# A hybrid decoder block on one core: mean squares from the transposed x, two u blocks in turns, first loads over two queues, scan states with tokens innermost

## The chip, the cores and the metric

One core of one Trainium2 chip runs the whole layer in one launch. The metric is the device time of that launch in microseconds (us), taken as the median of several runs.

## What is computed

The input is 256 tokens of 2048 floats. One residual block and one expert block follow:

```
h = rms_norm(x, attn_norm_g)
proj = h @ w_in[l]                      # u_ssm 1024, q, k, v 1024 each, two gates 2048 each
y_ssm = s5_mixer(u_ssm, ...)            # 64 groups of 16 channels, one complex diagonal state of 64 each,
                                        # bu = u @ bbar; x[t] = abar * x[t-1] + bu[t]; y = Re(c x) + d u
y_att = stick_breaking_attention(rms_norm(q), rms_norm(k), v)
merged = sigmoid(gate_ssm) * (y_ssm @ w_branch_ssm) + sigmoid(gate_att) * (y_att @ w_branch_att)
x = x + merged @ w_out
x = x + hierarchical_moe(rms_norm(x), ...)   # best of 4 groups, best 2 of its 8 experts; 32 experts of 2048 x 512
```

All numbers are float32. The norm divides by the root of the mean square of each token, so it can be applied to a product's rows after the matmul.

## The kernel before, in words

`hybrid_block` writes every engine's program in the order in which the engine runs it. The first part is a list of *blocks* (`b_orient`, `a_orient`, lines 209 to 246), one for 512 columns of a weight matrix: two of u, six of q, k, v, four of the attention gate, four of the attention branch, four of the other gate, two of the GLU, four of the ssm branch, four of the output. A block is cut into *chunks* of 256 of its rows (`subs`), 512 KB of weights each. For a chunk, `dma(i)` (line 124) loads it to `raw` by SP's queue, `split(i)` (line 131) makes two rounded parts of it: `wh` on ACT (a cast) and `wl`, the rest, on DVE. TensorE then multiplies three pairs (`wh` with `xh`, `wh` with `xl`, `wl` with `xh`), four matmuls of 512 columns each, so twelve a chunk. `xh` and `xl` are the same two parts of the transposed x times the norm's weight, made by `x_prep` (line 417). `raw`, `wh` and `wl` have three buffers each.

The loop at line 890 goes over the chunks: it splits chunk i+2, loads chunk i+5, issues the matmuls of chunk i and then lets side programs (generators) put their own instructions behind it, as long as a count of each engine's work allows. `later` puts something off by so many chunks. Four accumulators (`pacc`) serve two blocks at a time.

The side programs that the change touches are these.

- `init_stats` (line 458) makes `rstd`, one over the root mean square per token: it loads x a second time with tokens on the partitions (`xtok`, 2 MB by ACT's queue), squares it on ACT with a running sum, takes the root (`rsqrt`, line 192) and permutes the result by four small matmuls with `perm`, for the u blocks have even tokens in one accumulator and odd ones in the other (`rstdp`). The u blocks are evicted with it (`u_out`) and transposed (`u_tr`).
- `ssm` (line 510) computes the state's coefficients on POOL, clears two large tiles (`BBD`, `CBD`, lines 562 and 563), and fills them on DVE and ACT. It then multiplies u (pairs of tokens) into the states' inputs `Vs`, and after the scan it multiplies the states with `CBD` into `y` (lines 687 to 706): sixteen rounds, each four matmuls with `CB` and eight with `Vs` as the moving side, four column groups of 32 side by side.
- `scan` (line 489) runs over 128 token pairs on DVE. A step is one product and two additions for each of two halves, 64 and 32 elements per partition.

The tile of the states, and the moving side that the y matmuls read from it:

```
Vs = [unit(7 + h, [P, P, 2, 16], F32, f"Vs{h}") for h in range(2)]
pe.matmul(ps[js, 0:P], CBD[:, si - 1, 4 * b + j], X[:, :, si - 1, i],
```

The first P is the partition, the second the token pair, then real and imaginary, then 16 groups. In the preamble (lines 425 to 442) SP issues g1, the first parts of x and the first chunks in turns, and TensorE runs 30 transposes (`W0`) to be warm.

After the blocks come the router and the experts: 32 experts of 12 MB each, in pieces of 2 MB, by SP's queue into a ring of tiles that the first part frees (`load_piece`, line 839).

Of the kernel before, what the change touches and what calls it, by code (L numbers as in the profile page):

```python
# [9 lines left out]
F32 = mybir.dt.float32  # L10
# [7 lines left out]
P = 128  # L18
# [5 lines left out]
BIG = 1.0e4  # L24
U_LATE = (4, 2)
SHORT = 0.1
# [56 lines left out]
def hybrid_block(ctx, tc, A, out):  # L83
# [12 lines left out]
    def slot(h, shape, dt, name):  # L96
        return hp.tile(shape, dt, name=name, tag=f"h{h}")
# [33 lines left out]
    def split(i):  # L131
        if i >= len(subs):
# [20 lines left out]
    rbias = cp.tile([P, 36], F32, name="rbias")  # L153

    ident = cp.tile([P, P], F32, name="ident")
    make_identity(nc, ident)
    nc.scalar.dma_start(small, A["lamdt"])
    ones = cp.tile([P, P], F32, name="ones")
    pool.memset(ones, 1.0)
    uge = cq.tile([P, P], F32, name="uge")  # L160
# [209 lines left out]
    ssq = cp.tile([P, 2, 4], F32, name="ssq")  # L370
    tiny = cq.tile([P, 1], F32, name="tiny")

    def out_fin(n):
# [37 lines left out]

    for bi, (src, nk, begin, mm, fin) in enumerate(blocks):
        for s in range(nk // 2):
            subs.append((src, s, nk, begin, mm, fin))


    def x_prep(k0):
        for k in range(k0, k0 + 2):
            act.activation(xh[:, k], xT[:, k], AF.Copy, scale=g1[:, k:k + 1])
            vec.scalar_tensor_tensor(xl[:, k], xT[:, k], g1[:, k:k + 1], xh[:, k], op0=OP.mult, op1=OP.subtract)  # L420
# [8 lines left out]
    dma(1)  # L429
    x_load(4, 8)  # L430
    dma(2)
    x_load(8, 12)
    wps = acc_tile()
    for _ in range(W0):
        pe.transpose(wps[:, 0:P], ident, ident)
    x_prep(0)
    split(0)
    dma(3)
    x_load(12, 16)
    x_prep(2)  # L440
    split(1)
    dma(4)
    BC = unit(8, [P, 8, 32, 16], F32, "BC")
    xtok = unit(3, [P, 2, D], F32, "xtok")

    def side_loads():
        sp.dma_start(BC[:, 0:4], A["bc"])
        sp.dma_start(dsk, A["ssm_d"])
        sp.dma_start(qkg, A["qkg"])
        sp.dma_start(g2, A["g2"])  # L450
        sp.dma_start(wrg, A["wr"])
        sp.dma_start(rbias, A["rb"])
        prog["side"] = True

    rtmp = cq.tile([P, 3, 2], F32, name="rtmp")
    rsq = cq.tile([P, 2, 2], F32, name="rsq")

    def init_stats():
        yield 0
        for j in range(4):  # L460
            nc.scalar.dma_start(xtok[:, j // 2, 1024 * (j % 2):1024 * (j % 2) + 1024],
                                A["x"][j // 2][:, 1024 * (j % 2):1024 * (j % 2) + 1024])
            yield 0
        for j in range(4):
            xs = xtok[:, j // 2, 1024 * (j % 2):1024 * (j % 2) + 1024]
            act.activation(xs, xs, AF.Square, accum_out=rsq[:, j // 2, j % 2:j % 2 + 1])
            if j % 2:
                yield 0
        vec.tensor_reduce(rtmp[:, 0], rsq, axis=AX.X, op=OP.add)
        vec.tensor_scalar(rtmp[:, 1], rtmp[:, 0], 1.0 / D, EPS, op0=OP.mult, op1=OP.add)  # L470
        rsqrt(rstd, rtmp[:, 1], rtmp[:, 2])
        side_loads()
        yield -1
        for t in range(2):
            ps = bg_tile(t)
            for i in range(2):
                pe.matmul(ps[:, 0:1], perm[i][:, t], rstd[:, i:i + 1], start=(i == 0), stop=(i == 1))
            vec.tensor_copy(rstdp[:, t:t + 1], ps[:, 0:1])
        prog["rstd"] = True
        yield 0  # L480
# [780 lines left out]
```

## Time and profile before

| | |
|---|---|
| median of 3 runs | 1581.26 us (1581.25 to 1585.3) |
| the profiled execution: its own time, its span | 1583.46 us, 1581.8 us |
| TensorE busy, DVE busy, ACT busy | 1269.7, 523.5, 450.8 us |
| bytes read from HBM | 515.24 MB, 327 GB/s over the span |

The span is what the profile covers of the execution; the rest lies around it. A busy TensorE is not TensorE at its best: matmuls overlap and their ends are modelled, so here the distance from one start to the next says more than a length. An fp32 matmul shows as two records, one with rounded operands as one. "Line 77" is the helper through which all instructions of DVE, ACT and TensorE go, so rows are told apart by their tiles.

### The profile page before, as it was taken

The page shows a single profiled execution, that of the slowest core. Times are in us where ns is not written, and L with a number is a line of the kernel's source. Part 1 is how long each engine was busy: PE and PEld are TensorE (multiplying, and loading weights), DVE is VectorE, ACT ScalarE, POOL GpSimd, SP SyncE. Part 2 cuts the span into 40 slices and gives each one's busy share as a digit, 9 for nine tenths or more (in the row PEclk, how much of TensorE's full clock was granted, in tenths as well). Part 3 has the DMA queues.
Part 4 walks back from the last instruction along what each step waited for, and adds up shares of the span by engine and source line. Part 5 has one row for each costly group of instructions (what it writes and reads, how often), then busy time and mean ns, then how long its engine had stood idle before and what let it go on. Part 6 is the DMA issues. An engine that isn't in the chain of part 4 may idle for free. (4 is left out here: it accounts for less than half of the span.)

```text
span 1581.8 us, 25130 instructions
## 1 busy us (share of the span) xinstructions
PE 1269.7 (80%) x10654; PEld 859.6 (54%) x10654; DVE 523.5 (33%) x1342; ACT 450.8 (28%) x769; POOL 42.9 (3%) x112
## 2 busy tenths in 40 slices
PE   8899999999999999977657657657757657657697
PEld 6778888888867888844323323323423323323364
DVE  5664877788845754312002002001002002002001
ACT  5455567554435443221110110110110110110101
POOL 8200000000000000000000000000000000000000
PEclk9999999999999999999987979887988988879899
DMA  8454655566654877899999999999999999999996
GB/s 288 160 161 150 196 155 157 163 193 188 200 183 174 278 265 270 320 410 428 428 426 428 426 426 428 426 426 428 428 426 428 426 427 428 427 426 427 427 427 243
DMA packets 64674, 518.99 MB, mean 328 GB/s; under 512 B 7856, under 2 KB 7856, under 8 KB 40880
## 3 DMA queue, kind: packets, MB, share of 16 engines
q1 hardware_dynamic: 63840, 515.22, 82.7%
q10 hardware_dynamic: 720, 2.15, 0.4%
q8 instruction: 85, 1.39, 0.4%
q14 instruction: 29, 0.24, 0.0%
HBM read 515.24 MB, written 2.10 MB: 327 GB/s over the span
## 5 line engine op out<-in xcount | busy, mean ns | idle before, releaser
L77 PE MATMUL acc<-ew,XY 128*32 128x256 f32 x4096 | 310.7, 456 | 171.7 <-DMA ew<-wgu 171.6
L77 PEld LDWEIGHTS acc<-ew,XY 128*32 128x32 f32 x4096 | 142.4, 126 | 323.3 <-DMA ew<-wgu 186.8
L77 DVE TENSOR_TENSOR wl<-raw,wh 128x1024 fp32r<-128x1024 f32 x200 | 244.4, 1225 | 162.6 <-ACT wh L77 159.1
L77 ACT CAST wh<-raw 128x1024 fp32r<-128x1024 f32 x200 | 209.1, 1051 | 188.2 <-PE acc L77 137.1
L77 DVE TENSOR_TENSOR sg<-sg,acc 128x128 f32<-128x128 f32 x32 | 9.2, 288 | 662.8 <-ACT sg L77 662.8
L77 PE MATMUL acc<-ew,hT 128*32 128x256 f32 (+1 forms) x2080 | 146.9, 431 | 70.8 <-DMA ew<-wd 39.3
L77 ACT COPY XY<-acc 32x256 f32<-32x256 f32 (+1 forms) x260 | 93.4, 359 | 207.3 <-PE acc L77 204.8
L77 PE MATMUL acc<-wh,xh 128*128 128x512 f32 x512 | 145.4, 401 | 3.2 <-ACT wh L77 3.2
L77 PEld LDWEIGHTS acc<-ew,hT 128*32 128x32 f32 x2080 | 73.9, 122 | 136.2 <-issue 50.1
L77 PE MATMUL acc<-wl,xh 128*128 128x512 f32 x512 | 140.7, 392 | 1.1 <-DVE wl L77 1.0
L77 PE MATMUL acc<-wh,xl 128*128 128x512 f32 x512 | 141.2, 393 | 0.0
L77 ACT ACTIVATE sg<-acc 128x128 f32<-128x128 f32 x32 | 8.9, 277 | 419.3 <-PE acc L77 419.3
L77 PEld LDWEIGHTS acc<-wl,xh 128*128 128x128 f32 x512 | 96.4, 189 | 23.0 <-DVE wl L77 2.8
L77 PEld LDWEIGHTS acc<-wh,xl 128*128 128x128 f32 x512 | 97.1, 190 | 20.9
L77 PEld LDWEIGHTS acc<-wh,xh 128*128 128x128 f32 x512 | 93.8, 190 | 22.6 <-ACT wh L77 4.6
L77 PE MATMUL acc<-XY,sc 128*128 128x512 f32 x128 | 62.4, 628 | 14.6 <-ACT XY L77 14.5
L77 PE MATMUL bga<-SL,x 128*128 128x128 f32 x512 | 63.5, 280 | 10.3 <-DVE SL L77 10.3
L77 PEld LDWEIGHTS bga<-SL,x 128*128 128x128 f32 x512 | 59.0, 192 | 22.9 <-DVE SL L77 15.9
L77 DVE TENSOR_TENSOR Vs<-Vs,prod 128x32 f32<-128x32 f32 x508 | 68.1, 189 | 0.0
L77 PE MATMUL acc<-wh,m 128*128 128x512 f32 x256 | 64.6, 392 | 0.0
L77 DVE TENSOR_TENSOR accv<-accv,acc 128x512 f32<-128x512 f32 x56 | 38.5, 688 | 78.1 <-PE acc L77 78.1
L77 PEld LDWEIGHTS acc<-wh,m 128*128 128x128 f32 x256 | 47.6, 188 | 9.5
(228 smaller groups left out, 979.8 us busy)
## 6 DMA issues: line engine op xcount, KB each, us to landing
ew<-wgu SPq DMA_DIRECT2D x123, 2048.0 KB, 39.1
ew<-wd SPq DMA_DIRECT2D x61, 2048.0 KB, 39.1
raw<-win SPq DMA_DIRECT2D x128, 512.0 KB, 4.2
raw<-wout SPq DMA_DIRECT2D x32, 512.0 KB, 4.2
ew<-wgu SPq DMA_DIRECT2D x20, 512.0 KB, 5.5
raw<-wba SPq DMA_DIRECT2D x16, 512.0 KB, 4.7
raw<-wbs SPq DMA_DIRECT2D x16, 512.0 KB, 5.1
raw<-wglu SPq DMA_DIRECT2D x8, 512.0 KB, 5.2
```

The costliest lines, as they stand in the source:

```text
L77: return f(out, *args, **kw)
```

## The change

Each part is in the diff below, which is cut to its core.

1. **Mean squares.** x is not loaded a second time. When `xh` and `xl` of four row blocks are made, ACT squares that part of the transposed x in place, and DVE adds up over the row blocks (`xsq`, three instructions over 8, 4 and 4 of the 16). After chunk 15 (step 14), twelve matmuls with `xsq` as the stationary side and a column of ones add up over the partitions, in both orders of tokens at once, so `perm` is gone. `rstd` and `rstdp` come from one chain.
2. **Turns.** The first twelve chunks go to the two u blocks in turns; then come the last two of each. `x_prep` and the loads of x follow every second chunk. `U_LATE` and the side loads change with it: BC comes in four pieces, and the small tensors earlier.
3. **First loads.** `ones` is made first, on DVE, and a first activation on it has ACT's table loaded; then ACT's queue issues g1, the two halves of the first chunk and `lamdt`, while SP's queue starts with x in halves. `wh` of the first chunk is made by DVE, half by half. The warming transposes are 22.
4. **States.** `Vs` becomes `[P, 2, 16, P]`: the token pairs are innermost. The scan, the eviction into `Vs` and the y matmuls index it accordingly.

```diff
-U_LATE = (4, 2)
+U_LATE = (2, 1)
...
-W0 = 30
+W0 = 22
...
+    ones = cp.tile([P, P], F32, name="ones")
+    vec.memset(ones, 1.0)
+    tiny = cq.tile([P, 1], F32, name="tiny")
+    act.activation(tiny, ones[:, 0:1], AF.Copy)
     ident = cp.tile([P, P], F32, name="ident")
     make_identity(nc, ident)
-    nc.scalar.dma_start(small, A["lamdt"])
-    ones = cp.tile([P, P], F32, name="ones")
-    pool.memset(ones, 1.0)
...
-    perm = []
-    for i in range(2):
-        pt_ = slot(2 * i, [P, 2, P], F32, f"perm{i}")
-        pool.memset(pt_, 0.0)
-        for t in range(2):
-            pool.affine_select(out=pt_[:, t], in_=pt_[:, t], pattern=[[-2, P]], compare_op=OP.not_equal, fill=1.0,
-                               base=P * i - t, channel_multiplier=1)
-        perm.append(pt_)
...
+    turns = [(b, s) for s in range(6) for b in range(nu)] + [(b, s) for b in range(nu) for s in (6, 7)]
+    turns += [(b, s) for b in range(nu, len(blocks)) for s in range(blocks[b][1] // 2)]
+    for b, s in turns:
+        src, nk, begin, mm, fin = blocks[b]
+        subs.append((src, s, nk, begin, mm, fin))
...
-    sp.dma_start(g1, A["g1"])
-    x_load(0, 2)
-    dma(0)
+    raw0 = wp.tile([P, 2, 512], F32, name="raw", tag="raw")
+    src0 = subs[0][0]
+    nc.scalar.dma_start(g1, A["g1"])
+    x_load(0, 1)
+    nc.scalar.dma_start(raw0[:, 0], src0[:, 0])
+    x_load(1, 2)
+    nc.scalar.dma_start(raw0[:, 1], src0[:, 1])
+    dma(1)
...
+    hl_t[0] = tuple(wp.tile([P, 2, 512], F32R, name=n, tag=n) for n in ("wh", "wl"))
+    for k in range(2):
+        x_one(k)
+        vec.tensor_copy(hl_t[0][0][:, k], raw0[:, k])
+        vec.tensor_tensor(hl_t[0][1][:, k], raw0[:, k], hl_t[0][0][:, k], op=OP.subtract)
...
-        sp.dma_start(BC[:, 0:4], A["bc"])
...
+        elif k < 5:
+            sp.dma_start(BC[:, k - 1], A["bc"][:, k - 1])
+        else:
+            sp.dma_start(wrg, A["wr"])
...
+    xsq01 = slot(0, [P, 2, T], F32, "xsq01")
+    xsq = [xsq01[:, 0], xsq01[:, 1], slot(1, [P, T], F32, "xsq2")]
...
-        for j in range(4):
-            nc.scalar.dma_start(xtok[:, j // 2, 1024 * (j % 2):1024 * (j % 2) + 1024],
-                                A["x"][j // 2][:, 1024 * (j % 2):1024 * (j % 2) + 1024])
-            yield 0
-        for j in range(4):
-            xs = xtok[:, j // 2, 1024 * (j % 2):1024 * (j % 2) + 1024]
-            act.activation(xs, xs, AF.Square, accum_out=rsq[:, j // 2, j % 2:j % 2 + 1])
...
+        for at, j, red in ((4, 0, None), (6, 1, (0, 0, 8)), (9, 2, (1, 8, 12)), (12, 3, (2, 12, 16))):
...
+            act.activation(xT[:, 4 * j:4 * j + 4], xT[:, 4 * j:4 * j + 4], AF.Square)
+            if red:
+                vec.tensor_reduce(xsq[red[0]], xT[:, red[1]:red[2]].rearrange("p k t -> p t k"), axis=AX.X, op=OP.add)
+            side_load(1 + j)
...
+        ps = bg_tile(0)
+        for o in range(2):
+            for t in range(2):
+                tt = slice(t, T, 2) if o else slice(P * t, P * t + P)
+                for j in range(3):
+                    pe.matmul(ps[:, 2 * o + t:2 * o + t + 1], xsq[j][:, tt], ones[:, 0:1], start=(j == 0), stop=(j == 2))
+        vec.tensor_scalar(rtmp[:, 1], ps[:, 0:4].rearrange("p (o t) -> p o t", o=2), 1.0 / D, EPS, op0=OP.mult, op1=OP.add)
+        rsqrt(rtmp[:, 0], rtmp[:, 1], rtmp[:, 2])
+        vec.tensor_copy(rstd, rtmp[:, 0, 0])
+        vec.tensor_copy(rstdp, rtmp[:, 0, 1])
...
-                pe.matmul(ps[:, 0:1], perm[i][:, t], rstd[:, i:i + 1], start=(i == 0), stop=(i == 1))
...
-                vec.tensor_tensor(prod[h], X[:, c - 1][:, :, None, :].to_broadcast([P, 2, 2, 16]), coef[h], op=OP.mult)
+                vec.tensor_tensor(prod[h], X[:, :, :, c - 1][:, :, None, :].to_broadcast([P, 2, 2, 16]), coef[h], op=OP.mult)
...
-                    vec.tensor_tensor(X[:, c], X[:, c], prod[h][:, k], op=OP.add)
+                    vec.tensor_tensor(X[:, :, :, c], X[:, :, :, c], prod[h][:, k], op=OP.add)
...
-        Vs = [unit(7 + h, [P, P, 2, 16], F32, f"Vs{h}") for h in range(2)]
+        Vs = [unit(7 + h, [P, 2, 16, P], F32, f"Vs{h}") for h in range(2)]
...
-                src = tiles[i].rearrange("p (a r c) -> p c r a", a=2, r=2)
+                src = tiles[i].rearrange("p (a r c) -> p r a c", a=2, r=2)
...
-                act.copy(Vs[b // 4][:, :, :, j:j + 3:2], src)
+                act.copy(Vs[b // 4][:, :, j:j + 3:2], src)
...
-                            pe.matmul(ps[js, 0:P], CBD[:, si - 1, 4 * b + j], X[:, :, si - 1, i],
+                            pe.matmul(ps[js, 0:P], CBD[:, si - 1, 4 * b + j], X[:, si - 1, i],
...
-                            pe.matmul(ps[js, 1:P], CBD[:, 1 + si, 4 * b + j], X[:, 0:P - 1, si - 1, i],
+                            pe.matmul(ps[js, 1:P], CBD[:, 1 + si, 4 * b + j], X[:, si - 1, i, 0:P - 1],
...
-        if i < 6:
-            x_prep(2 * i + 4)
         split(i + 2)
         dma(i + 5)
+        if i < 12 and i % 2:
+            x_prep(i + 3)
+        if i % 2 == 0 and i < 8:
+            x_load(i + 8, i + 10)
```

How the mean squares move on DVE, at the chunks where rstd is made. `wl` is a chunk's second part, `rtmp` and `rstd` the chain of the norm, `xsq` the new sums. Before:

```order
L77 SCALAR_TENSOR_TENSOR xl<-xT,g_108,xh 128x256 x2
L77 TENSOR_TENSOR wl<-raw,wh 128x1024 x3
L77 TENSOR_REDUCE rtmp<-rsq 128x2
L77 TENSOR_SCALAR rtmp<-rtmp 128x2
L77 RECIPROCAL rstd<-rtmp 128x2
L77 TENSOR_TENSOR rtmp<-rstd 128x2
```

and now:

```order
L77 TENSOR_REDUCE xsq_222<-xT 128x256
L77 TENSOR_TENSOR wl<-raw,wh 128x1024
L77 RECIPROCAL sm<-sm 128x32
L77 TENSOR_TENSOR wl<-raw,wh 128x1024
L77 TENSOR_SCALAR rtmp<-bga 128x4
L77 RECIPROCAL rtmp<-rtmp 128x4
```

The chain of the norm has moved behind the coefficients' reciprocal (`sm`), and starts from a PSUM tile, `bga`, which the matmuls fill.

How TensorE's part of it moves. Before, behind chunk 10:

```order
L77 MATMUL acc<-wl,xh 128x512 x4
L77 MATMUL bga<-rstd,perm_133 128x1
L77 MATMUL bga<-rstd,perm_141 128x1
L77 MATMUL bgb<-rstd,perm_133 128x1
L77 MATMUL bgb<-rstd,perm_141 128x1
L77 MATMUL acc<-wh,xh 128x512 x4
```

and now, behind chunk 15:

```order
L77 MATMUL acc<-wl,xh 128x512 x4
L77 MATMUL bga<-ones,xsq_221 128x1 x2
L77 MATMUL bga<-ones,xsq_222 128x1
L77 MATMUL bga<-ones,xsq_221 128x1 x2
L77 MATMUL bga<-ones,xsq_222 128x1
L77 MATMUL bga<-ones,xsq_221 128x1 x2
L77 MATMUL bga<-ones,xsq_222 128x1
L77 MATMUL bga<-ones,xsq_221 128x1 x2
L77 MATMUL bga<-ones,xsq_222 128x1
L77 MATMUL acc<-wh,xh 128x512 x2
```

Four matmuls that wait for rstd are gone, twelve that wait for the sums are there.

What stands on DVE behind the chain of the norm, where `BC` and `BBD` are the state's coefficients and `uy` the transposed u. Before (wrg had come earlier, and two more copies of uy come later):

```order
L77 COPY uy<-bga 128x512
L77 TENSOR_TENSOR wl<-raw,wh 128x1024
L77 COPY uy<-bgb 128x512
L77 TENSOR_TENSOR wl<-raw,wh 128x1024
L77 TENSOR_TENSOR BC<-BC,sm 128x512 x2
L77 TENSOR_TENSOR BC<-BC 128x512
L77 TENSOR_TENSOR BC<-BC,sm 128x512 x2
L77 TENSOR_TENSOR BC<-BC 128x512
L77 TENSOR_TENSOR wl<-raw,wh 128x1024
```

and now:

```order
L77 TENSOR_TENSOR wrg<-wrg,g_113 128x576
L77 TENSOR_SCALAR qkg<-qkg 128x1
L77 TENSOR_TENSOR BC<-BC,sm 128x512 x2
L77 TENSOR_TENSOR BC<-BC 128x512
L77 TENSOR_TENSOR BC<-BC,sm 128x512 x2
L77 TENSOR_TENSOR BC<-BC 128x512
L77 TENSOR_TENSOR wl<-raw,wh 128x1024
L77 TENSOR_TENSOR BC<-BC,sm 128x512 x2
L77 TENSOR_TENSOR BBD<-BC 64x32x16 x2
L77 TENSOR_TENSOR wl<-raw,wh 128x1024
L77 COPY uy<-bga 128x512
```

wrg has come down to the coefficients, and all four copies of uy stand behind the first of them.

## Rows read from the trace of the kernel before

**Rows 1.** The page: head, and costliest groups (busy us, mean ns, idle before).

```profile
span 1581.8 us, 25130 instructions
...
L77 DVE TENSOR_TENSOR wl<-raw,wh 128x1024 fp32r<-128x1024 f32 x200 | 244.4, 1225 | 162.6 <-ACT wh L77 159.1
```

**Rows 2.** Stretches: us, PE, PEld, DVE, ACT, POOL busy, PEclk, DMA share, GB/s.

```profile
456.00:485.30 29.30, 29.30 (x386) 10.56 (x385) 7.00 (x11) 9.63 (x24) 0.00 (x0) 1.00 0.14 48
485.30:650.00 164.70, 164.47 (x867) 141.08 (x864) 92.87 (x101) 74.87 (x99) 0.00 (x0) 1.00 0.76 263
...
700.00:1500.00 800.00, 524.13 (x5917) 267.76 (x5909) 73.72 (x139) 97.22 (x282) 0.00 (x0) 0.86 1.01 427
```

**Rows 3.** The same table for the stretch of the scan.

```profile
147.00:447.40 300.40, 300.40 (x1375) 250.44 (x1374) 242.82 (x915) 166.09 (x193) 0.00 (x0) 1.00 0.59 183
```

**Rows 4.** Timeline, 35 to 50 us: start, us, engine, line, operation, count [idle before].

```profile
35.87 1.09 PE L77 MATMUL acc<-wh,xl 128*128 128x512 f32 x4
35.94 0.15 DVE L77 TENSOR_REDUCE rtmp<-rsq 128x2 f32<-128x4 f32 x1
36.12 5.63 DVE L77 TENSOR_SCALAR rtmp<-rtmp 128x2 f32<-128x2 f32 x1
...
36.80 1.10 PE L77 MATMUL acc<-wl,xh 128*128 128x512 f32 x4
...
38.22 3.51 POOL L563 MEMSET CBD<- 128x4096 f32 x1
...
43.13 0.98 PE L77 MATMUL bga<-rstd,perm 128*128 128x1 f32 x4 [5.23 <-DVE rstd L77]
...
44.83 2.05 PE L77 MATMUL acc<-wh,xh 128*128 128x512 f32 x4
...
49.43 1.09 PE L77 MATMUL acc<-wh,xh 128*128 128x512 f32 x4
```

**Rows 5.** Timeline, all engines, the first 9 us (same columns).

```profile
4.74 1.28 ACT L77 ACT_TABLE_LOAD   x1 [4.74 <-DMA xT<-xT]
...
7.93 1.20 PE L77 MATMUL acc<-wh,xh 128*128 128x512 f32 x4 [1.67 <-ACT wh L77]
```

**Rows 6.** Timeline of PE, the y stage.

```profile
456.03 0.42 PE L77 MATMUL bga<-uy,CB 32*32 32x128 f32 x8
456.38 1.55 PE L77 MATMUL bga<-Vs,CBD 128*32 128x128 f32 x16
457.87 0.42 PE L77 MATMUL bga<-uy,CB 32*32 32x128 f32 x8
...
485.30 2.18 PE L77 MATMUL acc<-zz,wh 128*128 128x256 f32 x16
```

**Rows 7.** Groups by shape: busy us, mean ns of one, idle before.

```profile
L77 PE MATMUL bga<-Vs,CBD 128*32 128x128 f32 x128 | 12.4, 531 | 0.0
...
L77 PE MATMUL bga<-SL,x 128*128 128x128 f32 x512 | 63.5, 280 | 10.3 <-DVE SL L77 10.3
...
L77 DVE TENSOR_TENSOR Vs<-Vs,prod 128x32 f32<-128x32 f32 x508 | 68.1, 189 | 0.0
...
L77 DVE TENSOR_TENSOR prod<-Vs,coef 128x64 f32<-128x64 f32 x254 | 45.0, 219 | 0.0
...
L77 ACT COPY Vs<-bga 128x512 f32<-128x512 f32 x8 | 4.8, 597 | 18.2 <-PE bga L77 18.2
...
L77 ACT COPY BT<-bga 128x512 f32<-128x512 f32 x4 | 2.4, 588 | 1.6 <-PE bga L77 1.6
```

**Rows 8.** Waits of PE from 50 to 640 us: us in total, times, longest.

```profile
PE acc L77 <- DVE wl L77: 1.0, 3, 0.4
PE acc L77 <- ACT wh L77: 0.6, 1, 0.6
```

**Rows 9.** Timeline of PE, the first expert.

```profile
663.53 1.93 PE L77 MATMUL acc<-ew,XY 128*32 128x256 f32 x32
665.39 3.84 PE L77 MATMUL bga<-SL,x 128*128 128x128 f32 x32
```

More of the change, by code (lines that the diff above doesn't have):

```diff
@@ L273, in hybrid_block @@
         b_orient(A["win"][n], 16, lambda k: xh[:, k], lambda k: xl[:, k], u_fin(n), par=True)
+    nu = len(blocks)
     S = {}
@@ L370, in hybrid_block @@
     ssq = cp.tile([P, 2, 4], F32, name="ssq")
-    tiny = cq.tile([P, 1], F32, name="tiny")
     def out_fin(n):
@@ L410, in hybrid_block, with x_one @@
         b_orient(A["wout"][n], 16, lambda k: S["m"][k // 8][:, 0, k % 8], lambda k: S["m"][k // 8][:, 1, k % 8], out_fin(n))
-    for bi, (src, nk, begin, mm, fin) in enumerate(blocks):
-        for s in range(nk // 2):
-            subs.append((src, s, nk, begin, mm, fin))
+    turns = [(b, s) for s in range(6) for b in range(nu)] + [(b, s) for b in range(nu) for s in (6, 7)]
[3 more added lines that the diff above has]
+        subs.append((src, s, nk, begin, mm, fin))
+    def x_one(k):
+        act.activation(xh[:, k], xT[:, k], AF.Copy, scale=g1[:, k:k + 1])
+        vec.scalar_tensor_tensor(xl[:, k], xT[:, k], g1[:, k:k + 1], xh[:, k], op0=OP.mult, op1=OP.subtract)
     def x_prep(k0):
         for k in range(k0, k0 + 2):
-            act.activation(xh[:, k], xT[:, k], AF.Copy, scale=g1[:, k:k + 1])
-            vec.scalar_tensor_tensor(xl[:, k], xT[:, k], g1[:, k:k + 1], xh[:, k], op0=OP.mult, op1=OP.subtract)
+            x_one(k)
     def x_load(k0, k1):
         sp.dma_start(xT[:, k0:k1], A["xT"][:, k0:k1])
-    sp.dma_start(g1, A["g1"])
-    x_load(0, 2)
-    dma(0)
+    raw0 = wp.tile([P, 2, 512], F32, name="raw", tag="raw")
[6 more added lines that the diff above has]
+    dma(1)
     x_load(2, 4)
-    dma(1)
-    x_load(4, 8)
     dma(2)
-    x_load(8, 12)
+    dma(3)
+    x_load(4, 6)
     wps = acc_tile()
@@ L435, in hybrid_block @@
         pe.transpose(wps[:, 0:P], ident, ident)
[L436 to L440, printed above, removed]
+    nc.scalar.dma_start(small, A["lamdt"])
+    hl_t[0] = tuple(wp.tile([P, 2, 512], F32R, name=n, tag=n) for n in ("wh", "wl"))
+    for k in range(2):
+        x_one(k)
+        vec.tensor_copy(hl_t[0][0][:, k], raw0[:, k])
+        vec.tensor_tensor(hl_t[0][1][:, k], raw0[:, k], hl_t[0][0][:, k], op=OP.subtract)
     split(1)
     dma(4)
+    x_load(6, 8)
+    x_prep(2)
@@ L443, in hybrid_block, with side_load @@
     BC = unit(8, [P, 8, 32, 16], F32, "BC")
-    xtok = unit(3, [P, 2, D], F32, "xtok")
-    def side_loads():
-        sp.dma_start(BC[:, 0:4], A["bc"])
[L448 to L456, printed above, removed]
+    def side_load(k):
+        if k == 0:
+            sp.dma_start(dsk, A["ssm_d"])
+            sp.dma_start(qkg, A["qkg"])
+            sp.dma_start(g2, A["g2"])
+            sp.dma_start(rbias, A["rb"])
+        elif k < 5:
+            sp.dma_start(BC[:, k - 1], A["bc"][:, k - 1])
+        else:
+            sp.dma_start(wrg, A["wr"])
+            prog["side"] = True
@@ L458, in init_stats @@
+    rtmp = cq.tile([P, 3, 2, 2], F32, name="rtmp")
+    xsq01 = slot(0, [P, 2, T], F32, "xsq01")
+    xsq = [xsq01[:, 0], xsq01[:, 1], slot(1, [P, T], F32, "xsq2")]
     def init_stats():
         yield 0
-        for j in range(4):
-            nc.scalar.dma_start(xtok[:, j // 2, 1024 * (j % 2):1024 * (j % 2) + 1024],
-                                A["x"][j // 2][:, 1024 * (j % 2):1024 * (j % 2) + 1024])
-            yield 0
-        for j in range(4):
-            xs = xtok[:, j // 2, 1024 * (j % 2):1024 * (j % 2) + 1024]
-            act.activation(xs, xs, AF.Square, accum_out=rsq[:, j // 2, j % 2:j % 2 + 1])
-            if j % 2:
-                yield 0
@@ L469, in init_stats @@
[L469 to L472, printed above, removed]
-        yield -1
-        for t in range(2):
-            ps = bg_tile(t)
-            for i in range(2):
-                pe.matmul(ps[:, 0:1], perm[i][:, t], rstd[:, i:i + 1], start=(i == 0), stop=(i == 1))
-            vec.tensor_copy(rstdp[:, t:t + 1], ps[:, 0:1])
-        prog["rstd"] = True
@@ L480, in init_stats @@
-        yield 0
+        for at, j, red in ((4, 0, None), (6, 1, (0, 0, 8)), (9, 2, (1, 8, 12)), (12, 3, (2, 12, 16))):
+            while prog["step"] < at:
+                if prog["step"] == 2 and "sl" not in prog:
+                    prog["sl"] = True
+                    side_load(0)
+                yield 0
+            act.activation(xT[:, 4 * j:4 * j + 4], xT[:, 4 * j:4 * j + 4], AF.Square)
+            if red:
+                vec.tensor_reduce(xsq[red[0]], xT[:, red[1]:red[2]].rearrange("p k t -> p t k"), axis=AX.X, op=OP.add)
+            side_load(1 + j)
+            yield 0
@@ new lines, in init_stats @@
+        while prog["step"] < 14:
+            yield 0
+        side_load(5)
+        ps = bg_tile(0)
[5 more added lines that the diff above has]
+        vec.tensor_scalar(rtmp[:, 1], ps[:, 0:4].rearrange("p (o t) -> p o t", o=2), 1.0 / D, EPS, op0=OP.mult, op1=OP.add)
@@ L481, in init_stats @@
+        rsqrt(rtmp[:, 0], rtmp[:, 1], rtmp[:, 2])
+        vec.tensor_copy(rstd, rtmp[:, 0, 0])
+        vec.tensor_copy(rstdp, rtmp[:, 0, 1])
+        prog["rstd"] = True
+        yield -1
         vec.tensor_tensor(wrg, wrg, g2[:, :, None].to_broadcast([P, 16, 36]), op=OP.mult)
```

## The prediction

> **What bounds the kernel now.** Read the page's head first: 1581.8 us of span [rows 1]. The table of stretches then splits it in two. From 700 to 1500 us the DMA engines are busy all the time at 427 GB/s [rows 2]: the expert weights stream, and TensorE waits for them. Before that TensorE is the bound: from 147 to 447 it is busy 300.4 of 300.4 us [rows 3], and from 485.3 to 650 it is busy 164.47 of 164.70 with DMA at a share of 0.76 [rows 2]. The expert stream is issued at fixed places of TensorE's program and into buffers that its program frees, so a microsecond taken from TensorE before 650 should start the stream, and so end the kernel, a microsecond earlier. The question is what the change takes from TensorE. Two places matter.
>
> The first is the start. A chunk of a weight block is twelve matmuls; three groups of four at 0.93 us (35.87 to 36.80 [rows 4]) make 2.80 us. The first chunk begins at 7.93, after ACT had sat until 4.74 for the first x and then loaded a table for 1.28 us [rows 5]. Ten chunks should end 28.0 us later, at 35.9; the tenth ends at 37.73 (36.80 + 0.93), 1.8 us late. Then TensorE does nothing for the blocks until 44.83. The chain is in [rows 4]: a TENSOR_SCALAR of two elements on DVE takes 5.63 us and ends at 41.75, just when the second of POOL's large memsets ends (41.73); rstd hangs on it, TensorE waits 5.23 us for rstd, and eight records of the permutation fill 43.13 to 44.83. The next chunk runs from 44.83 to 49.43, 4.60 us, at half the clock (the four matmuls take 2.05 instead of 1.1). The loss from 7.93 to 49.43 is 41.5 - 11 x 2.80 = 10.7 us.
>
> The second is the y stage, 456 to 485.3, with nothing but y's matmuls [rows 2, 6]. A round is eight CB records (456.03 to 456.38, 0.35 us) and sixteen Vs records (456.38 to 457.87, 1.49 us); an fp32 matmul leaves two records, so that is four matmuls in 0.35 but eight in 1.49, 0.74 per four. One Vs record takes 531 ns, while a matmul of 128 columns by 128 rows with an unbroken moving side (SL,x) takes 280 [rows 7]. The Vs moving side is read with 32 floats between tokens; everything else about it has quick neighbours in the trace.
>
> **The change part by part.**
>
> Start. The first x and the first weights come in halves over two queues, the table is loaded early, and DVE makes the first wh. g1 now stands behind the table load (1.28 [rows 5]) on ACT's queue, so it cannot be much earlier than before, and DVE must do six operations for two halves before the second half is split: two xl, two casts, two wl of half the size of a 1.23 us wl [rows 1]. I put the first matmul at 6.3, with a wait for the second half, and the end of chunk one at 10.0 against 10.73 (7.93 + 2.80): **-0.7** (from -1.8, if nothing waits, to +0.5, if the halves share bandwidth with the second weights). Eight fewer warming transposes cost nothing while they end less than the present 1.67 us ahead of the first matmul [rows 5].
>
> The 2 MB of token-major x are no longer loaded, and the turns between the two u blocks ask for x half as fast. The 1.8 us late by chunk ten go: **-1.8**. What is added in their place is BC in four pieces and small loads, earlier than before; a late one would be seen as TensorE waiting for wh.
>
> The mean squares now end in matmuls behind chunk 15, and the 5.63 us instruction has no successor in the memsets: a TENSOR_REDUCE ran beside that memset in 0.15 us [rows 4], and the first TENSOR_SCALAR of rstd comes near 52 us (10.0, fourteen chunks of 2.80, 2.6 of matmuls), when POOL's memsets (end 41.73, 1.7 us less of perm work ahead of them, lamdt asked for later) are done. The gap goes, 37.73 to 44.83: **-7.1**. The clock stays up, since nothing idles: 4.60 - 2.80, **-1.8**. The added matmuls are 12, so 24 records; eight (bga's four and bgb's) took 1.70 us at half clock [rows 4], 0.107 each at full: **+2.6**. Four squares on ACT replace four of the same size; four elements-by-token sums on DVE (2048, 1024 and 1024 elements, three instructions) are new, at a wl's rate 4.9 us, spread over ten chunks in which DVE has about 2.3 us free per pair of chunks: no cost, and at the worst rate of the rival below (8 us more) some 2 us.
>
> Behind chunk 15 comes a chain: matmuls, TENSOR_SCALAR, square root, seven small DVE operations of about 0.19 [rows 7], then the two evictions that free the accumulators for chunk 17, 0.6 each by ACT's copies of that size [rows 7]. With a hand-over of 0.1 at each change of engine I make it 3.4 us after the matmuls; chunk 16 covers 2.8: **+0.6**. From there to chunk 24 DVE was short already: TensorE waited 1.6 us in four waits [rows 8]. The order puts wrg (576 elements, 0.7) and two more copies of uy (512 elements, 0.6 each, by wl's rate) into that stretch, all ahead of wl chunks, and BBD's copies hold ACT's next cast until DVE is through: **+2.5** (0 to 4). Start in all: -5.7, between -9.5 and -2.
>
> The scan. 254 products and 508 additions [rows 7] now touch elements 512 bytes apart instead of neighbours. No row shows DVE doing this. The nearest is ACT, which writes Vs scattered: 597 ns for 512 elements, and 588 for BT, unbroken [rows 7]. I take it as free; any cost goes first into DVE's 57.6 idle us of this stretch [rows 3].
>
> y. With tokens innermost the moving side is unbroken. Per four Vs matmuls I take CB's 0.35, the nearest in columns and in the four column groups; 32 such groups give 32 x (0.74 - 0.35) = **-12.5**. The lower end is the experts' rate: 32 records of 256 columns in 1.86 us [rows 9], 0.47 per four matmuls, 0.24 for 128 columns: -16. If ACT's sixteen copies and the gelu between them come to decide a round of 1.05 us, some of it is given back; ACT is busy only 9.63 of the 29.3 us now [rows 2], so I expect little; -11.
>
> Sum: -5.7 - 12.5 = -18.2 from 1583.46, which is 1565.3; that execution stands 2.2 above the median of the runs, so **1563**. Its own range goes from 1555 (-9.5 - 16) to 1570 (-2 - 11, and a little DVE).
>
> Against this change speaks a rule on strides. The Trainium skill, Advanced Engine Details and Errata, section SBUF Cachelines, says that accesses which hit a new 16-byte line each time pay. By that rule, the trace agrees for TensorE's Vs reads (531 against 280 ns); for DVE no run here shows it, and there it would work against the new layout.
>
> **The rivals.**
>
> *DVE pays for the stride.* TensorE's excess is (531 - 280)/128 = 1.96 ns for each element out of line. On DVE that is 64 reads in a product, 125 ns x 254 = 32 us, and 32 reads and 32 writes in an addition, 125 ns x 508 = 64 us: 96 us into 57.6 idle ones. TensorE would then wait some 38 us for wl: 1563 + 38 = **1601**, slower. It decides once a scan step (127 of them) costs 0.6 us more ((57.6 + 18.2)/127); with reads alone (64 us) the end is near 1570 still. For it: TensorE's rows. Against: ACT's scattered writes, and that DVE takes 189 ns for 32 elements, mostly fixed.
>
> *The stride is not what slows y*: 128 rows, 32-wide column groups, or accumulation in one bank do. Then only the start remains, 1581.3 - 5.7 = **1576**. Against: the experts do 128 rows in 32-wide groups at 0.24 [rows 9].
>
> *The start gives nothing*: the halves land late, the clock drops in the wait between them (a chunk at half clock cost 1.8), and the DVE backlog behind chunk 15 takes the rest: only y's 12.5, **1569**.
>
> **How the numbers follow.** Forecast 0.75, DVE's stride 0.07, y unchanged 0.08, start lost 0.10. The range 1555 to 1574 holds the forecast and the lost start. No difference means within 0.3%, 4.7 us, about what a measurement can tell: faster lies below 1576.5. The third case sits on that border and is halved: faster 0.75 + 0.10 + 0.04 = 0.89, same 0.04, slower 0.07.
>
> **What would show it.** In the changed profile: the first chunk ending near 10, no gap of TensorE between 10 and 50 beyond the xsq matmuls, granted clock 1.00 throughout the first 50 us; no DVE instruction of 5 us; waits for wh and wl of 3 to 5 us between 55 and 90; Vs,CBD records near 280 ns and the y stage 17 us long; scan additions still near 190 ns; the expert stream at 427 GB/s, beginning 18 us earlier. I am wrong if Vs additions exceed 300 ns, if the y stage stays above 25 us, or if the stream does not move with TensorE.

## The result, and the profile after

The changed kernel takes 1567.36 us in the median (four runs, 1567.0 to 1567.59), the kernel before 1583.17 on the same chip (1581.25 to 1585.3): a ratio of 0.9900, 95% interval 0.9882 to 0.9917. That is 15.8 us less, where 18.2 were forecast; the range held the time. The profiled execution of the changed kernel has an own time of 1567.53 us. From its page, the head and the two groups of the scan on DVE (busy us, mean ns of one, idle before):

```profile
span 1565.8 us, 25150 instructions
...
L77 DVE TENSOR_TENSOR Vs<-Vs,prod 128x32 f32<-128x32 f32 x508 | 76.9, 222 | 0.0
...
L77 DVE TENSOR_TENSOR prod<-Vs,coef 128x64 f32<-128x64 f32 x254 | 56.0, 262 | 0.0
```

The difference of the two spans, 16.0 us, splits without a rest if both timelines of TensorE are cut at the same work. Chunks 2, 11, 12, 17 and 25 start at 10.83, 44.83, 49.43, 64.25 and 89.89 before, and at 13.52, 38.96, 41.76, 58.50 and 88.11 now:

| piece | before | after | moved by | forecast |
|---|---|---|---|---|
| to chunk 2's start | 10.83 | 13.52 | +2.7 | -0.7 |
| chunks 2 to 10, and the gap behind them | 34.00 | 25.44 | -8.6 | -1.8 - 7.1 |
| chunk 11 | 4.60 | 2.80 | -1.8 | -1.8 |
| chunks 12 to 16, with the sums over xsq | 14.82 | 16.74 | +1.9 | +2.6 |
| chunks 17 to 24 | 25.64 | 29.61 | +4.0 | +0.6 + 2.5 |
| chunk 25 to y | 366.14 | 367.04 | +0.9 | 0 |
| the y stage | 29.27 | 14.88 | -14.4 | -12.5 |
| from y's end to the end of the span | 1096.5 | 1095.8 | -0.7 | 0 |

Two groups of u's transposes, 0.36 each, have moved from the fourth piece to the fifth, so these two are better read as +2.6 and +3.3. Nearly all of the net gain is in y. What the start won by the gap that is gone (10.4), it lost again, all but 0.9, in its first chunk, in the matmuls over xsq and behind chunk 16: y starts at 455.15 instead of 456.03, 0.9 us earlier, where 5.7 were forecast.

**The y stage.** The timeline of TensorE in the changed kernel (start, us, engine, line, operation, count), against [rows 6]:

```profile
455.15 0.42 PE L77 MATMUL bga<-uy,CB 32*32 32x128 f32 x8
455.50 0.64 PE L77 MATMUL bga<-Vs,CBD 128*32 128x128 f32 x16
456.07 0.42 PE L77 MATMUL bga<-uy,CB 32*32 32x128 f32 x8
...
470.03 2.18 PE L77 MATMUL acc<-zz,wh 128*128 128x256 f32 x16
```

The sixteen Vs records now fill 0.57 us (455.50 to 456.07), not 1.49; a round takes 0.92. The groups by shape give the record, against 531 ns in [rows 7]:

```profile
L77 PE MATMUL bga<-Vs,CBD 128*32 128x128 f32 x128 | 5.2, 279 | 0.0
...
L77 ACT COPY Vs<-bga 128x512 f32<-128x512 f32 x8 | 4.7, 587 | 18.2 <-PE bga L77 18.2
```

**The first chunk.** TensorE again, from the start:

```profile
1.41 4.95 PE L77 MATMUL acc<-ident 128*128 128x128 f32 x22 [1.41 <-POOL ident masks.py:199]
7.56 1.19 PE L77 MATMUL acc<-wh,xh 128*128 128x512 f32 x2 [1.20 <-DVE wh L77]
9.12 1.19 PE L77 MATMUL acc<-wh,xh 128*128 128x512 f32 x2 [0.37 <-DVE wh L77]
10.11 1.91 PE L77 MATMUL acc<-wh,xl 128*128 128x512 f32 x4
11.81 1.91 PE L77 MATMUL acc<-wl,xh 128*128 128x512 f32 x4
13.52 1.33 PE L77 MATMUL acc<-wh,xh 128*128 128x512 f32 x4
```

The first matmul starts at 7.56, not 6.3, and the chunk runs at about half pace: a group of four takes 1.70 us (10.11 to 11.81), where [rows 4] have 0.93. DVE's first cast, the `wh` of the first half, waits for the weights until 6.98:

```profile
6.98 0.43 DVE L77 CAST wh<-raw 128x512 fp32r<-128x512 f32 x1 [2.61 <-DMA raw<-win]
```

**Chunks 17 to 24.** TensorE's waits from 0 to 460 us, then its timeline and DVE's at the longest of them:

```profile
PE acc L77 <- DVE wl L77: 2.7, 2, 2.4
PE acc L77 <- DVE wh L77: 1.6, 2, 1.2
PE acc L77 <- POOL ident masks.py:199: 1.4, 1, 1.4
PE acc L77 <- ACT wh L77: 1.1, 1, 1.1
```

```profile
82.07 0.61 PE L77 MATMUL acc<-wh,xl 128*128 128x512 f32 x2
85.05 0.73 PE L77 MATMUL acc<-wl,xh 128*128 128x512 f32 x2 [2.37 <-DVE wl L77]
85.63 0.97 PE L77 MATMUL acc<-wh,xh 128*128 128x512 f32 x2
```

```profile
75.36 0.69 DVE L77 COPY uy<-bgb 128x512 f32<-128x512 f32 x1
75.96 0.68 DVE L77 COPY uy<-bga 128x512 f32<-128x512 f32 x1
76.56 1.29 DVE L77 TENSOR_TENSOR BC<-BC,sm 128x512 f32<-128x512 f32 x2
...
80.44 0.68 DVE L77 COPY uy<-bgb 128x512 f32<-128x512 f32 x1
81.04 1.28 DVE L77 TENSOR_TENSOR BC<-BC,sm 128x512 f32<-128x512 f32 x2
82.36 1.39 DVE L77 TENSOR_TENSOR CBD<-BC 64x512 f32<-64x512 f32 x2
83.77 2.36 DVE L77 TENSOR_TENSOR wl<-raw,wh 128x1024 fp32r<-128x1024 f32 x2
```

DVE has no pause here, and the late `wl` stands behind copies of `uy` and the coefficients. The stretches (us, PE, PEld, DVE, ACT, POOL busy, PEclk, DMA share, GB/s) show the backlog, its half clock, the scan and the expert stream:

```profile
85.00:90.00 5.00, 4.95 (x15) 3.91 (x16) 4.92 (x6) 3.26 (x4) 0.00 (x0) 0.66 0.64 206
148.80:451.00 302.20, 302.05 (x1381) 251.39 (x1381) 260.04 (x916) 165.42 (x192) 0.00 (x0) 1.00 0.59 183
...
700.00:1500.00 800.00, 528.19 (x5845) 268.88 (x5837) 73.75 (x139) 97.27 (x281) 0.00 (x0) 0.84 1.01 427
```

After the wait of 2.37 us the granted clock is 0.66 of full between 85 and 90, so part of that stretch runs at 1.2 instead of 2.4 GHz. In the scan DVE has 42.2 idle us left (302.20 - 260.04), where it had 57.6 [rows 3], and TensorE still hardly waits (302.05 of 302.20 us busy). The stream keeps its 427 GB/s, as in [rows 2].

### The profile page after: what moved, and what is told of

The parts are those of the page before. It is cut to its first block, busy times and chain, and to the rows that moved or that the text cites. A ratio compares the mean times of both kernels' runs of the same rounds, so it can differ in the third digit from the quotient of the medians.

```text
span 1565.8 us, 25150 instructions
## 1 busy us (share of the span) xinstructions
PE 1264.8 (81%) x10662; PEld 861.8 (55%) x10662; DVE 543.2 (35%) x1348; ACT 448.7 (29%) x764; POOL 43.1 (3%) x105
## 5 line engine op out<-in xcount | busy, mean ns | idle before, releaser
L77 PE MATMUL acc<-ew,XY 128*32 128x256 f32 x4096 | 304.2, 449 | 166.7 <-DMA ew<-wgu 166.7
L77 DVE TENSOR_TENSOR wl<-raw,wh 128x1024 fp32r<-128x1024 f32 (+1 forms) x201 | 243.9, 1217 | 143.8 <-ACT wh L77 142.8
L77 PE MATMUL acc<-ew,hT 128*32 128x256 f32 (+1 forms) x2080 | 157.0, 454 | 70.0 <-DMA ew<-wd 40.9
L77 DVE TENSOR_TENSOR Vs<-Vs,prod 128x32 f32<-128x32 f32 x508 | 76.9, 222 | 0.0
L77 PE MATMUL acc<-XY,sc 128*128 128x512 f32 x128 | 64.8, 649 | 14.7 <-ACT XY L77 14.6
L77 DVE TENSOR_TENSOR prod<-Vs,coef 128x64 f32<-128x64 f32 x254 | 56.0, 262 | 0.0
```

The source lines that it names most:

```text
L77: return f(out, *args, **kw)
```

## The experiments

The theories: **A**, all of y's gain is the states' layout, and it adds to the rest. On the first chunk: 22 warming transposes are too few. **C**, the 5.63 us of one small DVE instruction in [rows 4] are the two large memsets on POOL, not anything in the norm. **D**, the backlog of chunks 17 to 24 is the four copies of `uy`, which the turns let pile up behind the coefficients on DVE. **E**, what a strided operand costs is decided by whether neighbours share a line of 16 bytes; its rival is that it grows with the distance. Ratios stand against the kernel before, on the same chip.

### The layout alone, and all but the layout

The first kernel is the one before with the new states, the second the changed one with the old states (the lines with `X` and `src` go the same way):

```diff
-        Vs = [unit(7 + h, [P, P, 2, 16], F32, f"Vs{h}") for h in range(2)]
+        Vs = [unit(7 + h, [P, 2, 16, P], F32, f"Vs{h}") for h in range(2)]
```

> The kernel before with the states laid out with tokens innermost, and nothing else of the change. Theory A (the y matmuls' strided moving side cost the time, and it is worth its full price alone): the y stage falls from 29.3 to about 14.9 us, Vs,CBD records to about 272 ns, and the time is 14 to 15 us under the kernel before; the start stays as it was (TensorE idle 5.2 us for rstd). Rival (part of the y gain needs the rest of the change, or the slower scan, 222 instead of 189 ns an addition, costs TensorE waits here): under 10 us of gain, and waits for wl between 147 and 450.

> The changed kernel with the old state layout: mean squares, turns and first loads alone. Theory A (the start gains 10 us at the old gap and gives 9 back at its first chunk and at DVE's backlog): the y stage is 29.3 us again and begins near 455, and the time is within 2 us of the kernel before. Rival (the start is worth its forecast of 5 to 6 us, and the layout less than 12): 5 us or more under the kernel before.

The layout alone: 1570.19 us, 0.9911 (0.9894 to 0.9927), 13.5 less. y takes 14.77 us (457.93 to 472.70), additions 221 and products 262 ns, as in the changed kernel. All but the layout: 1580.95 us, 0.9985 (0.9975 to 0.9995), 2.8 less, with y at 29.27 and records of 531 ns. The two add up to 16.3, against 15.8 together. Theory A holds in the main: the y stage gains its 14.5 us by the layout alone. Both times lie just outside what it asked for (14 to 15 us, and within 2): in the first profile a half-clock chunk behind the gap took 5.26 us instead of 4.60 and y began 1.9 us later, and the rest of the change is worth 2.8 us, with an interval from 0.8 to 4.0.

### Thirty warming transposes

```diff
-W0 = 22
+W0 = 30
```

> The changed kernel with 30 warming transposes again instead of 22. Theory B (the first chunk runs at half clock because the transposes end before the clock has risen): the last transposes run at about 0.11 us each, chunk one takes under 3.5 us from its first matmul instead of 6, ends before 12 instead of 13.5, and the time falls by 1 to 2.5 us. Rival (the first chunk is slow because its halves arrive late, the number of transposes does not matter): chunk one ends at 13.5 or later, and the time is the changed kernel's or up to 2 us more.

1564.89 us, 0.9883 (0.9866 to 0.9899). TensorE's start there:

```profile
1.41 6.23 PE L77 MATMUL acc<-ident 128*128 128x128 f32 x30 [1.41 <-POOL ident masks.py:199]
7.88 0.71 PE L77 MATMUL acc<-wh,xh 128*128 128x512 f32 x2 [0.24 <-DVE wh L77]
9.49 0.71 PE L77 MATMUL acc<-wh,xh 128*128 128x512 f32 x2 [0.90 <-DVE wh L77]
10.04 1.08 PE L77 MATMUL acc<-wh,xl 128*128 128x512 f32 x4
10.96 1.09 PE L77 MATMUL acc<-wl,xh 128*128 128x512 f32 x4
11.90 1.09 PE L77 MATMUL acc<-wh,xh 128*128 128x512 f32 x4
```

The matmuls run at the full pace from the first (0.92 from 10.04 to 10.96), and chunk 2 starts at 11.90 instead of 13.52. From the first matmul the chunk takes 4.0 us, not under 3.5, for 0.90 us of waiting are in it. Over all profiles shown or told of here: with 30 transposes the first four matmuls ran at the full pace in each of seven, with 22 in one of five (the pair layout below). So the pace of the first chunk hangs on the transposes, but not alone: with 22 it differs from execution to execution, and the gain of 2.5 us in the median, whose interval overlaps that of the changed kernel, may be partly chance.

### The first chunk's order on DVE

With 30 transposes, both casts of the first chunk ahead of both `wl`:

```diff
+    x_prep(0)
     for k in range(2):
-        x_one(k)
         vec.tensor_copy(hl_t[0][0][:, k], raw0[:, k])
+    for k in range(2):
         vec.tensor_tensor(hl_t[0][1][:, k], raw0[:, k], hl_t[0][0][:, k], op=OP.subtract)
```

> The changed kernel with 30 warming transposes, and on DVE the two casts of the first chunk's halves ahead of its two wl (after both xl). Theory F (the second half waits in DVE's order, not for its data): the wait between the two halves of chunk one (0.4 to 1.4 us) falls under 0.3, chunk one ends 0.5 to 1 us earlier than with 30 transposes alone (11.9), and the time is 0 to 1 us under that kernel's 1564.9. Rival (the second half's data land late): the second cast waits for DMA, and chunk one ends as with 30 transposes alone.

Chunk 2 starts at 11.15 instead of 11.90, and the wait between the halves is 0.49 instead of 0.90; the second cast then waits 0.83 us for its half of the weights. So the late half has a share. That the order has one is not shown: one of the kernels below, with 30 transposes and the old order, has the same 0.49, and chunk 2 at 11.23. The time shows no gain either: 1565.77 us, 0.9887 (0.9871 to 0.9904), and y starts at 452.53, as with the other order (452.41).

### The memsets of the kernel before, moved

In the kernel before, the clearing of `BBD` and `CBD` goes ahead of the coefficients' chain on POOL; nothing of the norm is touched.

```diff
+        pool.memset(BBD.rearrange("p a b t c -> p (a b t c)"), 0.0)
+        pool.memset(CBD.rearrange("p a b c -> p (a b c)"), 0.0)
         lr, li, ldt = small[:, 0], small[:, 1], small[:, 2]
...
-        pool.memset(BBD.rearrange("p a b t c -> p (a b t c)"), 0.0)
-        pool.memset(CBD.rearrange("p a b c -> p (a b c)"), 0.0)
```

> The kernel before with POOL's two large memsets (BBD, CBD) put ahead of the chain of coefficients instead of behind it, nothing else. Theory C (the memsets alone held the two-element TENSOR_SCALAR for 5.6 us): that instruction takes about 0.2 us, TensorE's 5.2 us wait for rstd and the half clock behind it go, the y stage begins 6 to 9 us earlier and the time falls by 6 to 9 us. Rival (DVE was held by something else, such as ACT's table load or the late x): the instruction still takes over 3 us and the time stays within 2 us.

1579.4 us, 0.9975 (0.9965 to 0.9984), 4.3 less. DVE's timeline, POOL's and TensorE's:

```profile
5.70 6.99 DVE L77 TENSOR_SCALAR iotan<-iota 128x32 f32<-128x32 f32 x1 [5.59 <-POOL iota L184]
...
35.46 0.15 DVE L77 TENSOR_REDUCE rtmp<-rsq 128x2 f32<-128x4 f32 x1
35.65 0.17 DVE L77 TENSOR_SCALAR rtmp<-rtmp 128x2 f32<-128x2 f32 x1
```

```profile
5.68 3.52 POOL L551 MEMSET BBD<- 128x4096 f32 x1
9.14 3.52 POOL L552 MEMSET CBD<- 128x4096 f32 x1
```

```profile
12.78 1.91 PE L77 MATMUL acc<-wh,xl 128*128 128x512 f32 x4 [3.31 <-DVE wl L77]
```

The instruction of the norm is down to 0.17 us and its gap is gone. But another TENSOR_SCALAR, that of `iotan`, starts 0.02 us behind the first memset and ends at 12.69 with the second (9.14 + 3.52 = 12.66): 6.99 us for 32 elements. The hold has only moved, and TensorE waits 3.31 us for it in place of 5.23; the eight matmuls behind that wait run at half pace, and chunk 2 starts at 16.20 instead of 10.83. Theory C holds. From chunk 2 to chunk 12 the kernel wins 9.6 us (29.02 instead of 38.60), and 5.4 of them are lost again in the first chunk: so the gain came out below 6 to 9 us. It also says that the new mean squares were not needed to lose the gap: what they do is to come after the memsets. In the changed kernel the two memsets run from 41.65 to 48.64 beside `wl`, `xl` and `xsq` of the usual lengths (1.23, 0.88, 2.05 us), and no TENSOR_SCALAR or copy of DVE stands there.

The Trainium skill, SBUF — State Buffer, section Who interferes with whom, says that copies, casts and tensor_scalar can run in a mode in which DVE and GpSimd exclude each other at a pair of ports, the later one waiting until the other's instruction ends, and that a tensor_reduce never does. The traces agree, with 5.63 and 6.99 us against 0.15 for the reduce in [rows 4], which ran beside the first memset of the kernel before:

```profile
34.77 3.52 POOL L562 MEMSET BBD<- 128x4096 f32 x1
```

Both held instructions, begun beside the first memset, ended with the second: two memsets in a row let nothing of the kind in between them.

### The copies of uy on ACT

The changed kernel, with one engine exchanged:

```diff
-vec.tensor_copy(uS[:, 4 * c:4 * c + 4], ps
+act.copy(uS[:, 4 * c:4 * c + 4], ps
```

> The changed kernel with the four copies of the transposed u (uy from bga and bgb, 0.68 us each) on ACT instead of DVE. Theory D (DVE's backlog behind the coefficients makes the 2.4 us wait for wl near 85 us and the half clock behind it): DVE is 2.7 us lighter between 65 and 90, the wait falls under 0.5 us, the half clock there goes, the y stage begins 2 to 4 us earlier and the time falls as much. Rival (the late casts of wh on ACT, which wait for data and for BBD's copies, set it): the copies delay ACT's casts by as much as they free DVE, waits for wh take the place of waits for wl, and the time stays within 1 us.

1562.82 us, 0.9866 (0.9849 to 0.9882). From chunk 17's start to chunk 25's it takes 25.37 us (61.33 to 86.70), not 29.61; the longest wait for `wl` is 0.54, and the granted clock is 1.00 from 70 to 90. Theory D holds, but not for the whole 4.2 us. In this profile the matmuls of chunk 16 ran at a granted clock of 0.50 from 56.06 to 61.33, 2.4 us longer; so TensorE came late to the stretch, its wait for ACT's `wh` was 0.21 instead of 1.12, and y starts only 1.7 us earlier (453.48). Where chunk 16 ran at the full pace, the stretch takes 28.60 to 30.05 us with the copies on DVE (four profiles) and 26.14 and 26.21 with them on ACT (the two kernels with both mends below); where it was slowed, 27.74 and 27.76 against 25.37. Like against like, the copies are worth 2.4 to 3.9 us.

The half clock behind the long wait does not always come. Six profiles have the wait of 2.37 or 2.38 us; behind it three run at a granted clock of about 0.50 (the changed kernel, the pairs below, the first chunk's other order), and three, such as that with 30 transposes, have 1.00 and lose nothing more than the wait.

### Two and four groups innermost

The changed kernel, with the states as `[P, 2, 8, P, 2]` and as `[P, 2, 4, P, 4]`: from token to token TensorE goes 8 or 16 bytes, and DVE has two or four neighbours. The scan, the eviction and the order of the four coefficients go with it.

```diff
-        Vs = [unit(7 + h, [P, 2, 16, P], F32, f"Vs{h}") for h in range(2)]
+        Vs = [unit(7 + h, [P, 2, 8, P, 2], F32, f"Vs{h}") for h in range(2)]
```

> The changed kernel with the states as pairs of groups: two groups innermost, then tokens, so TensorE's moving side steps by 8 bytes and DVE touches pairs of neighbours 1024 bytes apart (order of the four coefficients exchanged to fit). Theory E (what counts is whether two accesses in a row fall into one line of 16 bytes): Vs,CBD records stay near 272 ns, the y stage at 15 us, and the scan goes back to about 189 and 219 ns; the time is the changed kernel's within 1 us, for DVE had room. Rival (any step but one float costs TensorE): records of 350 ns or more, y stage over 20 us, time 5 us or more above the changed kernel.

> The same with four groups innermost, so that the moving side steps by 16 bytes and DVE touches runs of four. Theory E: every read of the moving side falls into a new line, the records go back to about 530 ns, the y stage to 29 us, the time to 14 us above the changed kernel; the scan runs at about 189 and 219 ns. Rival (the cost grows with the distance): records between 272 and 530 ns, a y stage between 15 and 29 us.

The pairs: 1566.66 us, 0.9897 (0.9881 to 0.9914), y 15.15 us. The fours: 1573.1 us, 0.9935 (0.9919 to 0.9952), 5.7 above the changed kernel where theory E asked for 14, y 22.03 us. The groups by shape of the pairs, then of the fours:

```profile
L77 DVE TENSOR_TENSOR Vs<-Vs,prod 128x32 f32<-128x32 f32 x508 | 68.9, 191 | 0.0
...
L77 PE MATMUL bga<-Vs,CBD 128*32 128x128 f32 x128 | 5.3, 282 | 0.0
...
L77 ACT COPY Vs<-bga 128x512 f32<-128x512 f32 x8 | 4.9, 610 | 18.0 <-PE bga L77 18.0
```

```profile
L77 DVE TENSOR_TENSOR Vs<-Vs,prod 128x32 f32<-128x32 f32 x508 | 68.0, 188 | 0.0
...
L77 PE MATMUL bga<-Vs,CBD 128*32 128x128 f32 x128 | 8.8, 404 | 0.0
...
L77 ACT COPY Vs<-bga 128x512 f32<-128x512 f32 x8 | 8.6, 1072 | 13.0 <-PE bga L77 12.9
```

One record costs TensorE 279 ns at 4 bytes from token to token, 282 at 8, 404 at 16 and 531 at 128 [rows 7]. Nothing is lost at 4 and 8 bytes, where two reads or more fall into one span of 16; at 16 it costs, and at 128 more. So theory E fits the place where the cost begins, and its rival is right that it then grows. ACT, which writes the same tile, goes with E: 587 and 610 ns at 4 and 8 bytes, 1072 at 16. DVE too: 188 and 191 with four or two neighbours, 222 with none. By the rule on lines that the prediction cited (the Trainium skill, Advanced Engine Details and Errata, section SBUF Cachelines) two hits on a line are enough to hide its latency; the three engines agree on that point, and how much one hit a line costs, by engine, is in these rows.

### Both mends together

The changed kernel with the copies on ACT and 30 transposes, and the same with the pairs:

```diff
-W0 = 22
+W0 = 30
...
-vec.tensor_copy(uS[:, 4 * c:4 * c + 4], ps
+act.copy(uS[:, 4 * c:4 * c + 4], ps
```

> The changed kernel with both mends of the runs so far: the four copies of uy on ACT, and 30 warming transposes. The additive theory: chunks 17 to 24 take 25.4 us from chunk 17's start to chunk 25's, as with the copies alone (29.6 in the changed kernel), and the first chunk ends by 12 at a full clock, as with 30 transposes alone; y begins at 456.0 - 0.9 - 4.2 - 2.7 = 448.2 to 450, and the time is 1567.4 - 4.2 - 2.5 = 1560.7, against 1562.8 with the copies alone and 1564.9 with 30 transposes alone. The rival: an earlier u block only makes the wait for the coefficients or for x longer, so y begins at 452 as in both kernels alone and the time stays at 1562.8 or above.

> The kernel with both mends, and two of the sixteen groups innermost in the states (8 bytes from token to token), which alone brought the scan's additions back to 192 ns at the same TensorE time per record (275). The theory that the scan's extra 19.8 us of DVE are hidden: no difference from the kernel with both mends within 1 us, additions at 192 and products at 218 ns, the y stage 15 us. The rival: with TensorE further ahead of DVE the scan has begun to cost, and the time falls by 1 to 3 us below the kernel with both mends.

Both mends: 1561.6 us (1560.49 to 1561.97), 0.9856 (0.984 to 0.9873), the best version here and 5.8 below the changed kernel. The first chunk ends at 11.76, chunks 17 to 24 take 26.14 us, and y starts in the range that the sum of the two gave:

```profile
449.38 0.42 PE L77 MATMUL bga<-uy,CB 32*32 32x128 f32 x8
```

The transposes add 1.2 us to what the copies give, not 2.5; the intervals of the two kernels overlap, so that they add anything to the time is not shown. With the pairs it is 1561.98 us, 0.9862 (0.9845 to 0.9878), the same within the runs, though additions take 191 ns instead of 221. The 19.8 us that the new layout costs DVE in the scan (76.9 + 56.0 against 68.1 + 45.0 in [rows 7]) are hidden, also with TensorE further ahead.

## Why the prediction was right, and where it was off

- **What bounds the kernel**: right. TensorE sets the time up to the experts, and every shift of y's end came out at the end of the span to within 1.9 us: that distance is 1094.6 to 1096.7 us in all twelve profiles.
- **y, -12.5**: right in kind, too small. Of the two prices per four matmuls, CB's 0.35 and the experts' 0.24, the measured 0.285 (0.57 for eight) lies in the middle, which makes 32 x (0.74 - 0.285) = -14.6; the stage measured -14.4. ACT's copies did not come to decide.
- **The gap, -7.1, and the half-clock chunk, -1.8**: right, and the cause that the prediction read out of [rows 4] as a coincidence of ends was shown by the moved memsets. The TENSOR_REDUCE of 0.15 us that it cites ran beside the first memset, not the second; the argument stands. The new TENSOR_SCALAR takes 0.16 us at 55.80.
- **The 1.8 us late by chunk ten**: 0.2 are left (13.52 to 38.96, nine chunks of 2.80). Whether the load that is gone or the turns did it, no run separates.
- **The xsq matmuls, +2.6**: measured 2.66 (52.96 to 55.62). A cost behind them had no term: in three of the nine profiles that have them, part or all of chunk 16 runs at a granted clock of 0.50 and takes 4.15 to 5.27 us instead of 2.88, with no wait ahead of it. The changed kernel's own profile is not one of the three.
- **The first chunk, -0.7**: wrong in sign, +2.7. Two steps failed. "Eight fewer warming transposes cost nothing while they end less than the present 1.67 us ahead": they ended 1.20 ahead, and the chunk ran at half pace. Here it was not the idle time: the transposes themselves had not got the pace up, 22 took 4.95 us, 0.23 each, where 30 took 4.86 before. In two other profiles with 22 (4.35 and 4.17 us) the first matmuls ran faster, and the pace fell behind them. And "first matmul at 6.3, end at 10.0" fails without that: with 30 transposes chunk 2 starts between 11.15 and 11.90 in four profiles, later than the 10.83 of before, because in the changed kernel the first half of the weights is there only at 6.98 (DVE's first cast starts then) and DVE makes five small things in a row from there (`wh`, `wl`, `xl`, `wh`, `wl`).
- **The backlog, +2.5 (0 to 4), and the chain, +0.6**: right in place and size together: chunks 17 to 24 cost +3.3 beside the moved transposes. The chain is the smaller part: its evictions end at 58.79, 3.2 us after the matmuls over xsq, and chunk 16 covers 2.88 of them; chunk 17 follows without a wait and its first four matmuls take 1.14 us instead of 0.91. So some 0.2 are the chain's and 3.0 the backlog's. Not foreseen was its form: a single wait of 2.37 us, in place of three of at most 0.4 [rows 8], which brings the clock down in this profile (0.66); the prediction charged the half clock only to the old gap. That goes on into chunk 25 and is part of the +0.9 behind it, for which it had no term.
- **The scan, free**: free for the time, not for DVE: 33 ns an addition and 43 a product, 19.8 us against the 96 of the rival and the 57.6 of cover. The row on ACT that spoke for it was a poor witness: in the old layout ACT wrote two groups of one token, 8 bytes apart, in turn, not one element a line.
- **The rivals**: that DVE's stride decides fell by its size (33 ns, not 125). That the stride is not the cause of y fell by the layout alone. "The start gives nothing" was nearly true, with y 0.9 us earlier, but its 1569 took y at only 12.5.

The sum is 2.2 us from the difference of the spans by two errors of opposite sign: the start came out 4.8 worse (3.4 of it in the first chunk), y and what follows 2.6 better. That they nearly cancelled was luck.

## What to carry to other kernels

Price a strided operand on the engine that waits, and look which engine has cover: here 14 us of TensorE were bought with 20 us of DVE that nobody waited for, and two neighbours per line would have cost neither. When a small instruction takes microseconds, look for what ran on the other engine at its end, before rewriting what it computes: moving two memsets took away the same gap, and put a hold where they then stood. When work is shifted in order, what it is queued behind at its new place is a term of the sum, and a long wait can cost twice, if the clock falls behind it, as it did here in three profiles of six.

## What the runs showed that I had not expected

- The granted clock did not show the slow start. From 7 to 14 us the table of stretches gives the changed kernel a PEclk of 1.00, while four matmuls take 1.70 instead of 0.93 us; the distance between starts shows it, the column does not. Where the pace had been up and fell again, it does: 0.76 for the same stretch with the old layout and with the fours. So the column seems to miss a slow stretch as long as the pace has not risen before; only two profiles, this one and that with the copies on ACT, show it:

```profile
7.00:14.00 7.00, 6.07 (x14) 4.35 (x15) 5.69 (x9) 3.64 (x5) 3.46 (x7) 1.00 0.65 222
```

  So the prediction's test "granted clock 1.00 throughout the first 50 us" held and told nothing.
- The reductions over strided elements were dearer than a wl: the prediction had priced all three sums at a wl's rate, 4.9 us, where they took 8.0. A reduction of 1024 elements that lie 1024 bytes apart takes DVE 2040 ns, against 1210 for 1024 neighbours. The first makes 256 sums and the second 8, so how much of it is the stride is not shown. No wait of TensorE came of it:

```profile
L77 DVE TENSOR_REDUCE hst<-vq 128x8 f32<-128x1024 f32 x4 | 4.8, 1210 | 0.0
...
L77 DVE TENSOR_REDUCE xsq<-xT 128x256 f32<-128x1024 f32 x2 | 4.1, 2040 | 0.0
...
L77 DVE TENSOR_REDUCE xsq<-xT 128x256 f32<-128x2048 f32 x1 | 3.9, 3893 | 0.0
```

- ACT pays for writes 16 bytes apart: 1072 ns against 587 for the same 512 elements. Why TensorE pays 125 ns at 16 bytes and 252 at 128 stays open; no distance between them was run.
